# Three column groups of the input projection by seven products in a stage of their own, the second queries projected plainly, the bias table made beside x's norm

## The chip, the cores and the metric

The kernel runs on one core of one Trainium2 chip. The metric is the device time of one execution in microseconds (us), from the first to the last instruction and the little that lies around them; lower is better.

## What is computed

One transformer block on 512 tokens of width 2048, in float32. The part that matters here is the first projection and what reads it:

```python
h = rms_norm(x, norm_mix_pre)
proj = h @ w_in                       # 2048 x (q 1024, kv 6 x 256, gates 24, retention 4 x 1024)
k_cmp = compress_kv(kv6[:, :, 0], ...)   # a block MLP over 32 tokens, stride 16
v_cmp = compress_kv(kv6[:, :, 1], ...)
o_a = nsa_attention(q_a, k_cmp, v_cmp, k_slc, v_slc, k_win, v_win, gates, t5_bias)
o_r = retention(rope(q_r), rope(k_r), v_r) * silu(g_r)
mix = concat(o_a, o_r) @ w_out
x = x + rms_norm(mix); u = relu(rms_norm(x) @ w_up) ** 2; out = x + rms_norm(u @ w_down)
```

There are 8 attention heads in 2 key groups (4 heads each) and 4 retention heads. With 8 selected blocks of 64 the selected branch sees every valid key.

## The kernel before, in words

**Precision.** A float32 product is made of three fp32r matmuls: each operand is cut into a high part (a copy to fp32r on ScalarE) and a low part (source minus high part, on VectorE); `mm3` (L153 to L157) issues high x high, high x low, low x high into one PSUM bank. `split` (L141 to L144) makes the pair.

**Blocks and steps.** The projection is worked off in blocks of up to 512 output columns. A block has 8 steps (B = NSLAB = 8), one for each slab of 256 rows of the weight: a slab is fetched on the SP queue into `raw`, split into `whi`/`wlo`, and used in four pieces of six matmuls. `feat_major` (L202) keeps the weight stationary and streams 512 tokens; `tok_major` (L224) keeps the tokens stationary and streams the block's columns. Either way a block of 512 columns is 192 matmuls of 512 columns. The order of the blocks is that of `drv.steps`: the keys and values to be compressed (512 columns, `kv_done`), the selected and window keys (512, `k_done`), the first four query heads (512, `q_done(0)`), the window values (256, `v_done(1)`), then for each retention head a block of queries and keys and one of values and gates, with the last four query heads (512, `q_done(1)`) behind head 0 (L762 to L775).

**Side work.** Attention, retention and the compression are generators of small pieces, in one list (`Side`, L67; L780 to L791). Each unit has a first part (scores) and a second part (mix, outs). A call of `side.step()` makes one piece of the second part of unit b and one of the first part of a unit that may be at most one further, b + 1. The driver (L273) calls it between the pieces of a step: `two` at two of the four pieces of a step, `three` at three. A unit may wait for a block (`after(n)`: n blocks are behind). The table of L794 to L799 says up to which block the driver runs with which rate, and how many units must be through before the last step of that block: `side.drain` makes what is still missing, piece after piece, with no projection between.

```python
            if next(self.ga, "end") != "end":     # L86, first part; L97 the same for the second
                return True
    def drain(self, units=None, firsts=0):        # L106
        while self.b < (...) or self.a < firsts:
            assert self.step() or ...
```

An attention unit (`nsa_unit`, L557) takes two heads and a quarter i of the tokens (i = 0 to 3, 128 to 512 keys). Its scores are 5 pieces (6 in the last quarter): four score matmuls (L584) with scale and bias on VectorE (L585), maxima (L602 to L608), six exponentials with sums on ScalarE (L612). Its mix is i + 5 pieces: scaling of the probabilities on VectorE (L616 to L622), then for each 128 keys four transposes on TensorE (L647), their split (L648), and two pieces later the products with the values (L637). A retention unit has 10 pieces of scores and 11 of outs (L683 to L760). All engines take their instructions in the order in which they are issued.

**The rest around the change.** The stage before the blocks makes x's norm and its transposed halves `Hh`, `Hl` beside the block of selected values and gates (L400 to L435). The bias table (L453) comes as side work of the first block; `compress(0)` and `compress(1)` (L483) fetch their weights on the SP queue (L494). `load_bias` (L550) reads the table back in 8 DMAs of the POOL queue. The up and down projections already take seven products for eight (ORDER, ADD, SPLIT, `Feed`; L866 to L977): a `Feed` fetches quarters of the weight in halves of 512 KB, adds quarters on VectorE (L956) or by an accumulating DMA on POOL (L922), and splits each sum (L961 on ScalarE, L938 on VectorE); the sums of the activations are made once (`x1_sums`, L1059).

## Time and profile before

| what | value |
|---|---|
| median of 3 runs | 2201.61 us (2201.35 to 2202.2) |
| the profiled execution | 2200.95 us |
| its span, first to last instruction | 2199.0 us, 31984 instructions |
| outside the span | 1.95 us |
| mean granted TensorE clock | 0.994 |

PE is TensorE's matmuls, PEld its weight loads (they overlap matmuls), DVE VectorE, ACT ScalarE, POOL GpSimd, SP the queue that issues most DMAs. A busy PE counts every matmul from its start to its modelled end, and matmuls overlap: the pace is read from how many of them a stretch holds. L numbers are lines of the kernel before.

### The profile page before, as it was taken

The page shows a single profiled execution, that of the slowest core. Times are in us where ns is not written, and L with a number is a line of the kernel's source. Part 1 is how long each engine was busy: PE and PEld are TensorE (multiplying, and loading weights), DVE is VectorE, ACT ScalarE, POOL GpSimd, SP SyncE. Part 2 cuts the span into 40 slices and gives each one's busy share as a digit, 9 for nine tenths or more (in the row PEclk, how much of TensorE's full clock was granted, in tenths as well). Part 3 has the DMA queues.
Part 4 walks back from the last instruction along what each step waited for, and adds up shares of the span by engine and source line. Part 5 has one row for each costly group of instructions (what it writes and reads, how often), then busy time and mean ns, then how long its engine had stood idle before and what let it go on. Part 6 is the DMA issues. An engine that isn't in the chain of part 4 may idle for free.

```text
span 2199.0 us, 31984 instructions
## 1 busy us (share of the span) xinstructions
PE 2154.7 (98%) x12787; PEld 1910.5 (87%) x12787; DVE 1535.1 (70%) x1828; ACT 984.4 (45%) x1425; POOL 122.7 (6%) x139
## 2 busy tenths in 40 slices
PE   8999999999999999999999999999999999999995
PEld 7888878878788899999999999999888888888874
DVE  6213555554555533578988877777878999999996
ACT  5213343343232323485554555555664454445453
POOL 0000000000000000000000000000000000000011
PEclk9999999999999999999999999999999999999997
DMA  6543324322324334577877757676775757566684
GB/s 198 135 120 90 94 65 96 94 75 82 86 75 124 109 101 129 176 233 214 230 218 205 207 165 204 168 205 184 235 230 166 213 157 224 145 202 185 189 220 99
DMA packets 255462, 348.97 MB, mean 159 GB/s; under 512 B 16299, under 2 KB 166139, under 8 KB 254417
## 3 DMA queue, kind: packets, MB, share of 16 engines
q1 hardware_dynamic: 199472, 263.07, 38.0%
q0 software_dynamic: 29616, 42.96, 11.8%
q10 hardware_dynamic: 26226, 40.91, 5.1%
q8 instruction: 100, 1.64, 0.3%
q14 instruction: 48, 0.39, 0.1%
HBM read 305.14 MB, written 41.75 MB: 158 GB/s over the span
## 4 chain that ended last, share of the span: by engine, by line
PE 90%; DVE 5%; issue 1%; ACT 1%; DMA 1%; POOL 0%; SPq 0%; DVEq 0%; ACTq 0%; POOLq 0%
PE prod L157 17%; PE prod L155 17%; PE prod L156 17%; PE mm L155 11%; PE mm L157 11%; PE mm L156 11%; PE S L584 2%; DVE wlo L938 2%; PE PT L647 1%; PE S L707 1%; PE oT L742 1%; PE oT L502 1%; PE oT L155 1%; PE oT L156 1%; PE oT L157 1%
## 5 line engine op out<-in xcount | busy, mean ns | idle before, releaser
L961 ACT CAST whi<-Y 128x1024 fp32r<-128x1024 f32 x227 | 238.2, 1050 | 283.1 <-PE prod L157 117.6
L156 PE MATMUL prod<-wlo,Hh 128*128 128x512 f32 x896 | 349.4, 390 | 2.3 <-DVE wlo L938 2.1
L157 PE MATMUL prod<-whi,Hl 128*128 128x512 f32 x896 | 348.7, 389 | 0.0
L155 PE MATMUL prod<-whi,Hh 128*128 128x512 f32 x896 | 348.6, 389 | 0.0
L144 DVE TENSOR_TENSOR wlo<-raw,whi 128x1024 fp32r<-128x1024 f32 (+4 forms) x152 | 168.6, 1113 | 255.1 <-ACT whi L143 254.6
L961 ACT CAST whi<-low 128x1024 fp32r<-128x1024 f32 x215 | 226.4, 1054 | 265.1 <-PE prod L157 131.6
L938 DVE TENSOR_TENSOR wlo<-Y,whi 128x1024 fp32r<-128x1024 f32 x227 | 276.8, 1220 | 51.5 <-ACT whi L961 50.5
L938 DVE TENSOR_TENSOR wlo<-low,whi 128x1024 fp32r<-128x1024 f32 x215 | 262.1, 1221 | 55.9 <-ACT whi L961 55.0
L157 PE MATMUL prod<-Hh,wlo 128*128 128x256 f32 x1024 | 284.3, 278 | 5.1 <-DVE wlo L938 5.1
L155 PE MATMUL prod<-Hh,whi 128*128 128x256 f32 x1024 | 284.6, 278 | 0.3 <-ACT Hh L143 0.3
L156 PE MATMUL prod<-Hl,whi 128*128 128x256 f32 x1024 | 284.0, 277 | 0.9 <-DVE Hl L144 0.9
L143 ACT CAST whi<-raw 128x1024 fp32r<-128x1024 f32 (+4 forms) x152 | 145.6, 960 | 302.0 <-PE mm L156 147.9
L155 PE MATMUL mm<-whi,Hh 128*128 128x416 f32 (+4 forms) x704 | 262.3, 373 | 0.6 <-ACT Hh L143 0.5
L157 PE MATMUL mm<-whi,Hl 128*128 128x416 f32 (+4 forms) x704 | 248.1, 352 | 0.7 <-DVE Hl L144 0.7
L156 PE MATMUL mm<-wlo,Hh 128*128 128x416 f32 (+4 forms) x704 | 247.6, 352 | 0.0
L155 PE MATMUL mm<-Hh,whi 128*128 128x512 f32 x512 | 214.7, 419 | 0.1
L155 PE MATMUL prod<-sx,whi 128*128 128x256 f32 x768 | 212.0, 276 | 0.0
L156 PE MATMUL prod<-sx,whi 128*128 128x256 f32 x768 | 212.0, 276 | 0.0
L157 PE MATMUL prod<-sx,wlo 128*128 128x256 f32 x768 | 212.0, 276 | 0.0
L156 PEld LDWEIGHTS prod<-wlo,Hh 128*128 128x128 f32 x896 | 168.2, 188 | 40.1 <-DVE wlo L938 5.3
L157 PE MATMUL mm<-Hh,wlo 128*128 128x512 f32 x512 | 200.5, 392 | 0.0
L156 PE MATMUL mm<-Hl,whi 128*128 128x512 f32 x512 | 200.0, 391 | 0.0
(273 smaller groups left out, 3909.4 us busy)
## 6 DMA issues: line engine op xcount, KB each, us to landing
raw<-in_w_in SPq DMA_DIRECT2D x160, 256.0 KB, 3.1
low<-in_w_up SPq DMA_DIRECT2D x76, 512.0 KB, 4.3
Y<-in_w_up SPq DMA_DIRECT2D x64, 512.0 KB, 4.7
low<-in_w_down SPq DMA_DIRECT2D x64, 512.0 KB, 4.6
Y<-in_w_down SPq DMA_DIRECT2D x64, 512.0 KB, 4.6
Y<-ud SPq DMA_DIRECT2D x49, 512.0 KB, 8.0
ud<-Y ACTq DMA_DIRECT2D x77, 256.0 KB, 4.8
raw<-in_w_out SPq DMA_DIRECT2D x32, 416.0 KB, 3.5
```

The source lines that it names most:

```text
L143: nc.scalar.copy(hi, src)
L144: nc.vector.tensor_sub(lo, src, hi.bitcast(F32))
L155: nc.tensor.matmul(ps, ah, bh, start=first, stop=False, skip_group_check=more)
L156: nc.tensor.matmul(ps, ah, bl, start=False, stop=False, skip_group_check=more)
L157: nc.tensor.matmul(ps, al, bh, start=False, stop=last, skip_group_check=more)
L502: nc.tensor.matmul(hid[:65, :DK], kv[:, l:l + STRIDE * 64 + 1:STRIDE], w1s[l // 16][:, l % 16, :], start=l == 0, stop=l == CBLK - 1)
L584: nc.tensor.matmul(sps[:, :c + L], QT[g][:, h, qs], k, start=True, stop=True)
L647: nc.tensor.transpose(pt[:, e * P:(e + 1) * P], Pt[:, e, rows_of(j)], ident)
L707: nc.tensor.matmul(sps[:, :n], QK[:, 2 + d, rows_of(j)], QK[:, d, j * P:], start=d == 0, stop=d == 1)
L742: nc.tensor.matmul(o[:, :DR], AT[:, a0:a0 + P], vr[:, j, :], start=j == 0, stop=j == i)
L938: nc.vector.tensor_sub(lo, src, hi.bitcast(F32))
L961: nc.scalar.copy(hi, src)
```

## The change

The first three blocks of 512 columns (keys and values to be compressed; selected and window keys; the first four query heads) leave the list of blocks. They become a stage of their own, `groups`, between the window values and the first retention head: each group of 512 columns is two halves of 256 columns, the weight and the activations are cut in 2 x 2 quarters, and seven products of 48 matmuls of 256 columns take the place of eight. `Feed` (moved up, with parameters for its pool and offsets) feeds it. The sums of the activations are made by `in_sums`, on VectorE and ScalarE, beside the window values' block and the first products. The results go to DRAM (`pd`), and so do the values (`vd`); later they are read back on the POOL queue. The bias table is made right after the selected values. The second four query heads stay a plain block of 512, now behind retention head 1. The compression's weights go by POOL instead of SP; the list of side units and the driver's table are new. A wider tile for the split weights (`SL + 64`) and other padding go with it.

```diff
-    first = tok_outer(v0, NG * DK + 3 * HA, v_done(0))
-    kv0 = slabs_of(w_in, [(OFF_KV, 512)], pool_a)
+    first = tok_outer(v0, NG * DK + 3 * HA, v_done(0, lambda: xp.tile([P, S], F32R, name='vst')))
+    v1 = slabs_of(w_in, [(OFF_KV + 1280, 256)], pool_a)
...
     for _ in products:
         pass
+    bias_table()
     ectx.close()
+    xctx.close()
...
+    INC = [(OFF_KV, OFF_KV + 256), (OFF_KV + 512, OFF_KV + 1024), (0, 256)]
+    pd = dram.tile([len(INC), 2, P, SL], F32, name="pd")
+    iearly = [(0, 0), (1, 0), (0, 1), (1, 1), (2, 0), (0, 2), (2, 1)]
+    iphases += [(n, p, in_source(n)) for n in range(len(INC)) for p in ORDER if (n, p) not in iearly]
+    ifeed = Feed(iphases, more, 3, [], wp, in_place)
...
+        vs = [ip.tile([P, SL], F32, name="db", bufs=2)... for _ in range(2)]
+        yield from both(2, lambda c: less(vs[c], part(0, 1, c), part(1, 1, c)))
+        yield from both(4, lambda c: more_of(vs[c], sub, part(0, 0, c)))
+        yield from both(5, lambda c: more_of(vs[c], add, part(1, 0, c)))
+        yield from both(3, lambda c: less(vs[c], part(0, 0, c), part(0, 1, c)))
...
+            for s in range(2):
+                hi, lo = ifeed.slab()
+                for f in range(2):
+                    for kk in range(4):
+                        mm3(ps[:, f * 256:(f + 1) * 256], hi[:, kk, rows_of(f)], lo[:, kk, rows_of(f)],
+                            xh[:, k, :], xl[:, k, :], start, last, more)
+                    yield
...
+    drv.steps += tok_major(v1, 256, v_done(1, vst))
+    work = in_sums()
+    sums = lambda c: next(work, None) if c % 2 else None
+    drv.run(2, pump=sums)
+    drv.run(3, pump=sums)
+    ifeed.load(4)
...
+    for n, _ in enumerate(groups()):
+        if n % 2 or n % 8 == 0:
+            next(work, None)
...
-            nc.sync.dma_start(w1s[c], w1[0][c * 16 * P:(c + 1) * 16 * P, :].rearrange("(l p) n -> p l n", p=P))
+            nc.gpsimd.dma_start(w1s[c], w1[0][c * 16 * P:(c + 1) * 16 * P, :].rearrange("(l p) n -> p l n", p=P))
...
     def compress(i):
+        for _ in range(2 if i else 5):
             yield
...
         nc.scalar.copy(hs, hid[:65, :DK])
+        if not i:
+            compress_load(1)
+        else:
+            v_load()
         yield
...
+    def k_load():
+        nc.gpsimd.dma_start(kS[:, :, 32:], pd[G_K, 0].rearrange("p (g n) -> p g n", g=NG))
+        nc.gpsimd.dma_start(kW, pd[G_K, 1].rearrange("p (g n) -> p g n", g=NG))
+    def v_load():
+        for a, v in enumerate((Vh, Vl)):
+            nc.gpsimd.dma_start(v.rearrange("p t b n -> p (t b n)"), vd[a].rearrange("p t b n -> p (t b n)"))
+    def q_load():
+        QT[0] = ap.tile([P, 4, S], F32, name="qT", tag="qT")
+        for j in range(2):
+            nc.gpsimd.dma_start(QT[0][:, 2 * j:2 * j + 2, :].rearrange("p f n -> p (f n)"), pd[G_Q0, j])
...
-    drv.steps += feat_major(kv0, 4, kv_done)
-    proj([(OFF_KV + 512, 256), (OFF_KV + 1024, 256)], k_done)
-    proj([(0, 512)], q_done(0))
-    proj([(OFF_KV + 1280, 256)], v_done(1), tok=True)
     for h in range(HR):
         proj([(OFF_QR + h * DR, DR), (OFF_KR + h * DR, DR)], qk_done(h))
         proj([(OFF_VR + h * DR, DR), (OFF_GR + h * DR, DR)], vg_done(h), tok=True)
-        if h == 0:
-            proj([(512, 512)], q_done(1))
+        if h == 1:
+            proj([(512, 512)], q_done)
     B = NSLAB
     two = lambda c: side.step() if c % 2 else None
     three = lambda c: side.step() if c else None
+    every = lambda c: side.step()
     after = lambda n: (lambda: drv.at > n * B)
-    side.add(bias_table, nothing)
-    side.add(lambda: compress(0), nothing, after(1))
-    side.add(lambda: compress(1), nothing, after(1))
+    def loads():
+        k_load()
+        load_bias(0)
+        q_load()
+        for _ in range(6):
+            yield
+    side.add(lambda: compress(0), nothing)
+    side.add(lambda: compress(1), nothing)
+    side.add(loads, nothing)
     for u in range(8):
-        side.add(*nsa_unit(0, u // 2, u % 2), after(3), after(4))
-    side.add(*ret_unit(0), after(6))
+        if u == 4:
+            side.add(*ret_unit(0), after(2), after(3))
+        side.add(*nsa_unit(0, u // 2, u % 2))
+    side.add(*ret_unit(1), after(4), after(5))
     for u in range(8):
-        side.add(*nsa_unit(1, u // 2, u % 2), after(7))
-        if u == 5:
-            side.add(*ret_unit(1), after(9))
-    side.add(*ret_unit(2), after(10), after(11))
-    side.add(*ret_unit(3), after(12))
-    for blocks, units, firsts, pump in ((3, 3, 0, two), (4, 0, 0, two), (7, 10, 11, three), (8, 11, 12, three),
-                                        (9, 12, 12, three), (10, 12, 19, two), (11, 19, 19, two),
-                                        (12, 22, 22, three)):
+        if u == 4:
+            side.add(*ret_unit(2), after(7), after(8))
+        side.add(*nsa_unit(1, u // 2, u % 2), after(6))
+    side.add(*ret_unit(3), after(9))
+    kv_load()
+    compress_load(0)
+    for blocks, units, firsts, pump in ((2, 0, 0, every), (3, 0, 0, three), (4, 7, 8, three), (5, 8, 0, three),
+                                        (6, 11, 12, three), (7, 12, 13, three), (8, 13, 0, three), (9, 22, 22, three)):
         drv.run(blocks * B - 1, pump=pump)
         side.drain(units, firsts)
```

In the changed list the window values are block 0; the retention heads' and the second queries' blocks are 1 to 9 (queries and keys of head 0, its values and gates, the same of head 1, the second queries as block 5, then heads 2 and 3), and the output projection starts with block 10.

## Rows read from the trace of the kernel before

**Rows 1.** The page's first part (busy time, share of the span and number of instructions of each engine) and a group of weight loads from its fifth (count, then busy us, mean ns of one | idle before).
```profile
PE 2154.7 (98%) x12787; PEld 1910.5 (87%) x12787; DVE 1535.1 (70%) x1828; ACT 984.4 (45%) x1425; POOL 122.7 (6%) x139
...
L156 PEld LDWEIGHTS prod<-wlo,Hh 128*128 128x128 f32 x896 | 168.2, 188 | 40.1 <-DVE wlo L938 5.3
```
**Rows 2.** Busy time by stage (stretches): x's norm; the three blocks and the compression; the window values; the nine blocks with the side work; the output projection; up; down. Columns: stretch, its length, then busy us and (instructions) of each engine, granted clock, DMA share, GB/s.
```profile
0.00:48.80 48.80, 39.68 (x261) 35.23 (x262) 33.72 (x64) 28.61 (x66) 4.82 (x12) 1.00 0.63 202
48.80:198.60 149.80, 149.80 (x722) 123.53 (x721) 35.08 (x51) 31.96 (x44) 5.28 (x10) 1.00 0.44 118
198.60:222.70 24.10, 24.08 (x209) 23.88 (x207) 10.94 (x28) 11.62 (x36) 0.00 (x0) 1.00 0.43 121
222.70:749.90 527.20, 526.47 (x2485) 423.59 (x2486) 294.20 (x551) 182.97 (x393) 12.91 (x24) 1.00 0.32 90
749.90:936.70 186.80, 185.74 (x1021) 184.19 (x1020) 86.39 (x128) 67.97 (x126) 7.69 (x14) 1.00 0.42 129
936.70:1560.10 623.40, 617.38 (x5409) 616.44 (x5410) 504.66 (x504) 348.70 (x433) 42.80 (x36) 1.00 0.72 203
1560.10:2174.00 613.90, 611.55 (x2690) 503.66 (x2688) 560.59 (x487) 306.91 (x320) 42.22 (x36) 1.00 0.64 189
```
**Rows 3.** What the matmuls of the whole span waited for: us in total, times, longest.
```profile
PE prod L157 <- DVE wlo L938: 5.1, 3, 3.8
PE mm L331 <- DMA g<-in_norm_mix_pre: 3.9, 1, 3.9
PE PT L339 <- DVE h L355: 3.9, 3, 2.1
PE prod L156 <- DVE wlo L938: 2.1, 4, 1.2
PE oT L742 <- DVE rn L748: 0.7, 1, 0.7
```
**Rows 4.** Two stretches of 100 us with one shape of matmul each: 256 columns (up) and 512 columns (down); columns as in rows 2.
```profile
1200.00:1300.00 100.00, 100.00 (x883) 100.00 (x882) 80.35 (x82) 54.46 (x65) 7.63 (x6) 1.00 0.72 199
1700.00:1800.00 100.00, 100.00 (x443) 82.81 (x442) 94.57 (x83) 48.51 (x49) 7.09 (x6) 1.00 0.68 202
```
**Rows 5.** VectorE's groups of instructions in the up stage (936 to 1560 us), by shape: busy us, mean ns of one | idle before.
```profile
L938 DVE TENSOR_TENSOR wlo<-Y,whi 128x1024 fp32r<-128x1024 f32 x112 | 136.6, 1222 | 38.5 <-ACT whi L961 37.6
L956 DVE TENSOR_TENSOR Y<-Y,low 128x1024 f32<-128x1024 f32 x35 | 42.7, 1219 | 0.2
L1074 DVE TENSOR_TENSOR Y<-Y 128x1024 f32<-128x1024 f32 x8 | 9.7, 1218 | 0.0
```
**Rows 6.** VectorE's group of the window values' slabs (48.8 to 222.7 us), by shape.
```profile
L144 DVE TENSOR_TENSOR wlo<-raw,whi 128x512 fp32r<-128x512 f32 x8 | 5.5, 690 | 15.5 <-ACT whi L143 15.5
```
**Rows 7.** DMA issues of the whole program: queue, count, KB each, median us from issue to landing.
```profile
low<-in_w_up POOLq DMA_DIRECT2D x21, 512.0 KB, 7.6
BT<-rd POOLq DMA_DIRECT2D x16, 128.0 KB, 6.9
w1s<-in_cmp_w_k SPq DMA_DIRECT2D x2, 0.5 KB, 7.8
```
**Rows 8.** Two stretches by what the DMA engines did: the compression's second weights, and the bias read back beside a block's slabs; columns as in rows 2.
```profile
135.00:145.00 10.00, 10.00 (x50) 8.16 (x49) 1.23 (x1) 1.13 (x2) 0.00 (x0) 1.00 0.99 300
160.00:171.00 11.00, 11.00 (x52) 8.78 (x50) 3.19 (x9) 1.20 (x2) 3.98 (x8) 1.00 0.89 159
```
**Rows 9.** The POOL engine's groups of issues, of the whole span: busy us, mean ns of one | idle before.
```profile
L922 POOL DMA_DIRECT2D low<-in_w_up x21 | 26.7, 1272 | 319.6 <-ACT whi L961 132.1 <-DVE Y L956 82.4 <-DVE low L956 59.2
L553 POOL DMA_DIRECT2D BT<-rd x16 | 8.1, 515 | 280.0 <-DVE Pt L585 177.2 <-PE oT L502 102.8
L442 POOL DMA_DIRECT2D hot<-in_c_hot x1 | 0.6, 632 | 0.3 <-issue 0.3
```
**Rows 10.** One mix of the last quarter in order of time (start us, us, engine line operation), beside the scores of the next unit; the block's matmuls between them are left out.
```profile
608.00 0.18 DVE L616 RECIPROCAL nst<-nst 128x6 f32<-128x6 f32 x1
608.22 0.17 DVE L618 TENSOR_TENSOR nst<-nst,gat 128x6 f32<-128x6 f32 x1
608.42 1.68 DVE L622 TENSOR_SCALAR Pt<-Pt,nst 128x512 f32<-128x512 f32 x4
...
614.68 0.60 PE L647 MATMUL PT<-misc,Pt 128*128 128x128 f32 x4
615.12 1.02 PE L584 MATMUL S<-kT,qT 128*128 128x512 f32 x2
615.32 0.59 ACT L143 CAST ph<-PT 128x512 fp32r<-128x512 f32 x1 [2.50 <-PE PT L647]
615.93 0.69 DVE L144 TENSOR_TENSOR pl<-PT,ph 128x512 fp32r<-128x512 f32 x1 [1.61 <-ACT ph L143]
```
**Rows 11.** ScalarE's exponentials of the last quarter and the reads of their sums (400 to 749.9 us), by shape.
```profile
L612 ACT ACTIVATION_READ_ACCUMULATOR Pt<-Pt,nst 128x1 f32 x32 | 6.0, 186 | 0.0
L612 ACT ACTIVATE Pt<-Pt,nst 128x512 f32<-128x512 f32 x8 | 5.7, 710 | 0.0
L612 ACT ACTIVATE Pc<-Pc,nst 128x31 f32<-128x31 f32 x4 | 1.2, 311 | 0.0
```
**Rows 12.** VectorE's maxima of the last quarter and TensorE's side matmuls (500 to 749 us and 222.7 to 749.9 us), by shape.
```profile
L608 DVE TENSOR_REDUCE nst<-Pt 128x2 f32<-128x1024 f32 x2 | 2.4, 1220 | 0.1
L155 PE MATMUL oT<-ph,Vh 128*128 128x256 f32 x80 | 22.5, 281 | 0.0
```
**Rows 13.** A long wait of TensorE at the start of the up stage, and the stretch behind it; columns as in rows 2.
```profile
990.00:994.30 4.30, 0.48 (x5) 0.28 (x3) 4.30 (x5) 2.25 (x3) 0.71 (x1) 1.00 1.01 326
994.30:998.70 4.40, 4.40 (x25) 4.40 (x26) 4.38 (x4) 2.50 (x4) 1.92 (x2) 0.61 0.83 203
```

More of the change, by code (lines that the diff above doesn't have):

```diff
@@ L265, in block_kernel, with __init__, add, step @@
+    class Later:
+        def __init__(self):
+            self.at, self.todo = 0, []
+        def add(self, slabs, work):
+            self.todo.append((self.at + slabs, work))
+        def step(self):
+            self.at += 1
+            due = [w for n, w in self.todo if n <= self.at]
+            self.todo = [(n, w) for n, w in self.todo if n > self.at]
+            for w in due:
+                w()
     side = Side()
@@ L315, in block_kernel @@
     xts, hx, sx = {}, {}, {}
-    ones = ap.tile([1, P], F32, name="ones")
+    ones = xp.tile([1, P], F32, name="ones")
     nc.vector.memset(ones, 1.0)
@@ new lines, in groups @@
+    def groups():
+        sets = []
+        for i, (g, p, _) in enumerate(iphases):
+            n = g if isinstance(g, int) else g[0]
+            more = p in (1, 6)
+            if more:
+                ps = held_in.pop((n, p))
+            else:
+                ps = mm.tile([P, S], F32, name="mm")
+                if p in (0, 3):
+                    held_in[n, {0: 1, 3: 6}[p]] = ps
+            for s in range(2):
+                hi, lo = ifeed.slab()
+                if s == 0 and sets:
+                    in_done(*sets.pop())
+                ilater.step()
+                hi, lo = (v.rearrange("p (k n) -> p k n", k=4) for v in (hi, lo))
+                xh, xl = IA[p]
+                for f in range(2):
+                    for kk in range(4):
+                        k = 4 * s + kk
+                        o = ps[:, f * 256:(f + 1) * 256]
+                        start, last = k == 0 and not f and not more, k == 7 and f == 1
+                        mm3(o, hi[:, kk, rows_of(f)], lo[:, kk, rows_of(f)], xh[:, k, :], xl[:, k, :], start, last,
+                            more)
+                    yield
+            sets.append((n, p, ps))
+        yield
+        in_done(*sets.pop())
+        for _ in range(3):
+            ilater.step()
@@ new lines, in block_kernel, with vst @@
+    vsts = []
+    def vst():
+        if not vsts:
+            v = ip.tile([P, SL], F32R, name="vst", tag="da", bufs=3)
+            vsts.extend((v[:, :S], v[:, S:]))
+        return vsts.pop(0)
+    drv.steps += tok_major(v1, 256, v_done(1, vst))
[4 more added lines that the diff above has]
+    ifeed.load(4)
+    drv.run(len(drv.steps) - 2, pump=sums)
+    raws = [wr.tile([P, KC, S], F32, name="raw").rearrange("p k n -> p (k n)") for _ in range(3)]
@@ new lines, in block_kernel @@
+    ifeed.free += raws
+    for _ in range(3):
+        ifeed.advance()
+    drv.run(len(drv.steps) - 1, pump=sums)
+    drv.run()
+    next_up = slabs_of(w_in, [(OFF_QR, DR), (OFF_KR, DR)], pool_a)
+    for n, _ in enumerate(groups()):
+        if n % 2 or n % 8 == 0:
+            next(work, None)
+        if raws and not ifeed.loads and all(any(r is f for f in ifeed.free) for r in raws):
+            for i in range(3):
+                next_up[i].fetch()
+            raws = []
+        if ifeed.at == 2 * len(iphases) and not hasattr(next_up[0], "hi"):
+            next_up[0].load()
@@ L833, in block_kernel @@
     for s in range(NSLAB):
-        drv.run(12 * B + s + 1, pump=lambda c: side.first() if c % 2 else None)
+        drv.run(9 * B + s + 1, pump=lambda c: side.first() if c % 2 else None)
         if s:
@@ L839, in block_kernel @@
     mx.close()
-    drv.run(14 * B - 1, pump=lambda c: side.second() if c % 2 else None)
+    drv.run(11 * B - 1, pump=lambda c: side.second() if c % 2 else None)
     side.drain()
-    drv.run(16 * B)
+    drv.run(13 * B)
     rctx.close()
@@ L1128, in block_kernel @@
     phases += [(("down", c, nb), p, dn_source(c, nb)) for c in range(NCH) for nb in range(2) for p in ORDER]
-    feed = Feed(phases, [low0, low1], 3, [("down", NCH - 1, nb) for nb in range(2)])
+    feed = Feed(phases, halved(low0) + halved(low1), 3, [("down", NCH - 1, nb) for nb in range(2)], hp,
+                lambda g, p, s: 40 if isinstance(g, int) and p == 6 and s else 0)
     tmp = Ring(*xt, *(xh[:, c:c + 512] for c in range(0, 2048, 512)))
```

398 lines of the change are left out of this document (234 added, 164 removed).

## The prediction

> **What bounds the kernel now.** I read the page's first part, then the stages, then what TensorE waited for. Matmuls fill 98% of the span [rows 1], and between 48.8 and 2174 us no stage leaves TensorE idle by more than a per cent [rows 2]. In the nine blocks with the side work the only wait of a matmul that shows is 0.7 us, of a retention product; the longest of all lie at the starts of the norm and of the up stage [rows 3]. So attention's long chains cost TensorE's own time and nothing more: a piece always has a block's matmuls around it. The time therefore falls by what TensorE is spared, and rises by every place where it has to wait.
>
> **What the seven products save.** Three blocks are 3 x 192 = 576 matmuls of 512 columns; the new stage has 3 x 7 x 48 = 1008 of 256. Where one shape runs alone, 100 us hold 443 wide matmuls, 225.7 ns each, or 883 narrow ones, 113.3 ns each [rows 4]. 576 x 0.2257 = 130.0 us against 1008 x 0.1133 = 114.2 us: **15.8 us saved**. The old stage of 149.8 us [rows 2] is this 130.0 and the compression and table, which stay.
>
> The Trainium skill (TensorE: Matmul & The Clock Gate, section Back-to-back issue gap) speaks against this: it gives sustained spacings of 81 ns at 128 columns and 131 ns at 512. An estimate on a straight line between them is 98 ns at 256, so 98 us for the new stage against 75 for the old, a loss of 23 us, and a sum of 2257. The trace disagrees with that page: its narrow matmul costs half a wide one.
>
> **The sums of the activations.** `in_sums` is 28 VectorE pieces on 1024 elements, 1.22 us each as such pieces of the up stage [rows 5]. 16 lie beside the window values' block, whose 192 narrow matmuls last 21.7 us. VectorE owes in that time 16 x 1.22 = 19.5, six low parts of slabs at 0.69 = 4.1 [rows 6], two first low parts of the new stage, 2.4, and four low parts of values, about 1.7: 27.7 us. The third slab's low part ends at 28.9 and is wanted at 21.7 + 2 x 2.7 = 27.1, 1.8 us late. For the next five products a slab (24 matmuls, 2.7 us) carries one low part and 1.25 pieces, 2.75 us, so the delay neither grows nor shrinks much. The nearest row for such a start is that of the up stage, whose products waited 5.1 + 2.1 us for low parts [rows 3]. Bounds 0 and 7; I take **+4**, between the hand count and that row.
>
> **The read back.** Keys, queries and values were copied from PSUM into place; now they come from DRAM through POOL's queue, in issue order. `v_load` goes out with call 20 of the side work (13 pieces of `compress(0)`, 7 of `compress(1)`), `k_load`, the bias and `q_load` with call 24, and the first score matmul with call 30. One call per six matmuls: the cover is 10 x 6 x 0.2257 = 13.5 us. Ahead of the first queries lie 2.1 MB of values, 1.05 of keys, 1.05 of bias and 0.52 of queries. DMA engines that are full moved 300 GB/s; the bias took 11 us beside a block's slabs at 159 GB/s in all [rows 8], its issues 0.5 us each [rows 9], 6.9 us to landing [rows 7]. A block's slabs are 4.2 MB in 43 us, 97 GB/s, which leaves some 200. Upper end: 3.67 / 0.2 = 18.4, and 11 for the bias, less 13.5: 16. Lower end: all 4.7 MB at 300 GB/s, 15.7 less 13.5: 2. TensorE takes instructions in order, so this wait holds up the block behind it too. I take **+10**: the bias's slow pace is measured on this very transfer, while the slabs are fetched up to three ahead and can give way. The first compression's weights (1.05 MB each, 7.8 us to landing [rows 7]) have six to eight calls, 8 to 11 us, of cover; bounds 0 and 4, taken as 0.
>
> **The drain.** This is what decides. I walked the driver's loop call by call. In the old table every unit due at a `drain` is through: no piece is ever left over. In the new one nine blocks instead of twelve carry the side work, and two of them carry less than they could: in block 5 11 of 24 calls find nothing (the second queries are not there yet), in block 7 9 (head 2's outs wait for block 8). At block 8 the line is head 2's outs, 11 pieces; unit 14's mix, 7; unit 15's mix. 21 calls come before the drain, and 11 + 7 + 3 = 21. Left are 4 pieces of unit 15's mix, then 8 of unit 16's, one call for unit 16's change to unit 17, and 8 of unit 17's, with the scores of 16 and 17 beside them: **21 steps with no block's matmul between**, on the widest units there are.
>
> What TensorE waits for in them: from a unit's last score to its first transposition there are one maximum, 1.22 us [rows 12], six exponentials with the reads of their sums, 4 x (0.710 + 0.186) + 2 x (0.311 + 0.186) = 4.6 us [rows 11], and the scaling, 2.1 us [rows 10]: 7.9 us, with some 3 us of the other unit's pieces beside it. Twice, about 10 us. In the other pieces transpositions, high part and low part take 1.94 us (614.68 to 616.62) [rows 10], then six products of about 0.118 us (pace of the narrow matmul; 281 ns each if alone [rows 12]): 2.6 us for the two pieces that may be in flight, 1.3 each, against about 1.0 of TensorE's own. 0.3 x 20 = 6. Together **+16**. Lower end 8, when only one of the long waits shows; upper end 28, when no two pieces are in flight (14 x 1.3 = 18, and 10).
>
> **The clock.** A wait of 3.8 us in the up stage was followed by 4.4 us with a granted clock of 0.61, most of it at the lower of the two levels (1.2 of 2.4 GHz), holding 25 matmuls where the pace of rows 4 gives 39: 1.6 us lost [rows 13]. Three waits here are as long or longer. 3 x 1.6 = 4.8, but in the drain TensorE is not the bound: **+3**, bounds 0 and 5.
>
> **At nothing.** The bias table keeps its three products; its issues on POOL (0.6 us each [rows 9]) stand in front of the last root of x's norm there, under the selected values' products, 1.7 us if that cover is gone. The late sums are issues of 1.27 us on POOL [rows 9], 7.6 us to landing [rows 7], with three products, 16 us, ahead of their use. 36 halves of 0.52 MB, 3.1 MB of accumulation and 3.1 of stores in about 118 us are 213 GB/s, beside 203 at a DMA share of 0.72 in the up stage [rows 2]. SP, relieved of the compression's weights, had made nothing wait.
>
> **Sum.** Against the profiled execution's 2200.95 us (span 2199.0 and 1.95 around it; the median, 2201.61, is 0.7 higher): 2200.95 - 15.8 + 4 + 10 + 16 + 3 = **2218 us**.
>
> **Rivals.**
> 1. *The loads are hidden, the drain is not.* The number of empty calls of `compress` and `loads` speaks for it, the bias's 11 us against. Without the 10 and one clock drop: 2207. Chance 0.20.
> 2. *Faster: the leftover pieces run at TensorE's pace.* The place is the end of block 8. Unit 15's remainder and unit 16's pieces would have to cover unit 17's exponentials, and the loads to land in time; the price is then 2200.95 - 15.8 + 4 + 1 = 2190. It decides when the idle time of the drain and of the first score together stays under 10 us. For it: VectorE is busy for 56% of these blocks and ScalarE for 35% [rows 2]. Against: the chain is one of latencies, and needs 7.9 us whatever else is idle. Chance 0.11.
> 3. *The new stage starves.* Each group wants four halves at its second product, from eight buffers; in the up stage's start the long wait came with the DMA engines full, 326 GB/s [rows 13]. Three times 3.8 + 1.6 in place of 4: 2218 + 12 = 2230. Chance 0.08.
> 4. *The weight load paces the narrow matmul.* It is busy 100% of the narrow stretch, 83% of the wide [rows 4], and takes 188 ns [rows 1]. If two could not overlap: 1008 x 0.188 = 190 us, 2218 + 75 = 2293. 883 in 100 us exclude it where it was measured: 0.01. The spacings of the Trainium skill's page named above would be a milder form of it.
>
> **How the numbers follow.** The forecast has 0.59. The range, 2200 to 2238, reaches down over the first rival and the low ends and up over the third; below it lies most of the second, above it the sum of the upper ends (2241) and the fourth. A measurement of this kernel can tell some 0.2%, 4.4 us, from no change. Faster by more: rival 2, 0.12 with a remainder. Within: the lower half of rival 1, 0.10. Slower: the forecast, the upper half of rival 1, rivals 3 and 4, 0.78.
>
> **What would show it.** Right: the stage of the 1008 products lasts 114 to 122 us; a wait of TensorE of 5 to 15 us before the first L584-like score, released by a DMA; two waits of 4 to 6 us ahead of transpositions at the end of block 8, released by VectorE, and in that stretch a busy share near 0.6 and a dip of the granted clock. Wrong: a first score that waits under 2 us (rival 1); no stretch without block matmuls, or one under 25 us (rival 2); more than 10 us of waits for low parts in the new stage (rival 3).

## The result: slower by 1.1%

| | before | after |
|---|---|---|
| median of the compared runs | 2201.9 us (2201.35 to 2202.65, 4 runs) | 2226.72 us (2222.95 to 2228.86, 4 runs) |
| profiled execution, its span | 2200.95, 2199.0 us | 2225.34, 2222.9 us |

The ratio of the two versions' times is 1.0111, 95% interval [1.0093, 1.0128]. The profiled execution is 24.4 us longer than before; the forecast was 17 us. The saving came as predicted, the costs were larger and lay in part in other places.

The page's first part after, to be held against [rows 1]: TensorE has 432 instructions more, VectorE 82 us more to do, and the span grew.

```profile
PE 2156.9 (97%) x13219; PEld 1929.1 (87%) x13219; DVE 1617.3 (73%) x1907; ACT 1009.4 (45%) x1448; POOL 149.1 (7%) x171
```

The stages after, against [rows 2]: the norm, the window values, a short stretch at the new stage's start, the three groups, the nine blocks (the compression now in them), up, down; the output projection, left out, is as long as before. Columns as there: stretch, length, busy us and (instructions) of PE, PEld, DVE, ACT, POOL, granted clock, DMA share, GB/s.

```profile
0.00:49.50 49.50, 41.44 (x261) 37.12 (x262) 33.03 (x65) 27.88 (x66) 7.05 (x15) 1.00 0.63 188
49.50:72.90 23.40, 23.40 (x198) 22.29 (x197) 19.42 (x25) 7.88 (x12) 1.40 (x2) 1.00 0.81 233
72.90:78.00 5.10, 0.29 (x4) 0.09 (x2) 4.65 (x6) 4.03 (x7) 0.00 (x0) 0.79 0.68 209
78.00:196.90 118.90, 117.44 (x1009) 117.05 (x1010) 94.47 (x90) 49.72 (x53) 15.51 (x18) 0.98 0.73 191
196.90:770.90 574.00, 557.95 (x2640) 447.05 (x2640) 304.36 (x588) 190.40 (x424) 25.09 (x44) 0.98 0.36 104
...
957.70:1582.80 625.10, 618.83 (x5409) 617.89 (x5410) 504.94 (x504) 349.01 (x434) 42.98 (x36) 0.99 0.72 203
1582.80:2197.40 614.60, 611.78 (x2688) 503.43 (x2687) 560.50 (x487) 306.86 (x320) 42.45 (x36) 1.00 0.65 188
```

How the spans' 23.9 us come out of these stages. Before, everything from the norm's end to the output projection took 749.9 - 48.8 = 701.1 us; after, 770.9 - 49.5 = 721.4, so 20.3 more. The saving of 15.8 is in it, so 36.1 us were added. Values and groups should have taken 24.1 + 114.2 = 138.3 and took 147.4: **9.1**. Compression, table and nine blocks took 149.8 - 130.0 + 527.2 = 547.0 before, the last two of them 574.0 after: **27.0**. The other 3.6 us are 0.7 in the norm, 1.7 in up, 0.7 in down and 0.5 behind the last stage.

What the matmuls waited for, over the whole span, the longest groups (total, times, longest), against [rows 3]:

```profile
PE PT L973 <- DVE Pt L948: 5.5, 2, 3.1
PE prod L157 <- DVE wlo L339: 5.4, 3, 3.8
PE mm L155 <- DVE vst L144: 4.8, 1, 4.8
PE oT L813 <- ACT KV L809: 4.2, 1, 4.2
...
PE oT L1068 <- DVE rn L1074: 3.1, 4, 1.5
```

The `prod` waits are the up stage's, as before. Three others are new and long: 4.8 us for the values' split `vst`, 4.2 us for a copy into `KV`, and 5.5 us in two for the scaled probabilities `Pt` (L948 is L622 of the kernel before). No score (L910) waits long, neither for a DMA nor at its first place.

**The saving.** In the middle of the groups, one shape of matmul with its sums beside it:

```profile
115.00:175.00 60.00, 60.00 (x531) 60.00 (x530) 49.05 (x47) 24.50 (x25) 5.05 (x4) 1.00 0.79 212
```

531 in 60 us is 113.0 ns each, the up stage's pace of [rows 4]. The stage's 118.9 us are the 114.2 of the forecast, 1.5 of waits for low parts, 2.4 lost at its start, where 4.7 us of work ran at half the clock, and 0.8 that I cannot place.

**The start of the groups.** Around the 4.8 us wait, in order of time (start us, us, engine line operation, tiles, shape, count, [idle before <- releaser]); the value block's last matmul starts at 72.90:

```profile
72.43 2.35 DVE L339 TENSOR_TENSOR wlo<-half,whi 128x1024 fp32r<-128x1024 f32 x2
...
73.21 1.04 ACT L362 CAST whi<-half 128x1024 fp32r<-128x1024 f32 x1 [1.81 <-PE mm L157]
...
74.16 1.99 ACT L656 CAST sv<-db 128x1024 fp32r<-128x1024 f32 x2
75.23 2.36 DVE L658 TENSOR_TENSOR sv<-db,sv 128x1024 fp32r<-128x1024 f32 x2 [0.45 <-ACT sv L656]
76.06 1.19 ACT L143 CAST vst<-mm 128x256 fp32r<-128x256 f32 x4
77.51 1.41 DVE L144 TENSOR_TENSOR vst<-mm,vst 128x256 fp32r<-128x256 f32 x4
```

The first product of the groups needs a PSUM bank that still holds values. They were finished at 73 us, but ScalarE first made a slab half's high part and those of two sums (L656), VectorE the low parts of two halves and of the sums (L658), and only then came the values' own pair at 76.06 and 77.51; TensorE goes on at 77.98. The clock fell while it stood:

```profile
72.90:75.90 3.00, 0.28 (x3) 0.08 (x1) 2.55 (x3) 2.69 (x3) 0.00 (x0) 1.00 0.45 113
75.90:82.70 6.80, 4.71 (x22) 4.72 (x23) 6.80 (x10) 1.34 (x5) 2.84 (x4) 0.50 0.95 269
```

**The first compression.** ScalarE at 210 us, its next two instructions after one that ended at 200.3; L143 makes the high parts of the blocks' slabs, L809 copies the positions beside the keys, and TensorE's product L813 reads them:

```profile
209.99 1.04 ACT L143 CAST whi<-raw 128x1024 fp32r<-128x1024 f32 x1 [9.73 <-DMA raw<-in_w_in]
210.94 0.18 ACT L809 COPY KV<-PT 128x32 f32<-128x32 f32 x1
```

The first row is the point. ScalarE takes instructions in order; the cast stands for 9.7 us because its slab has not landed, and the copy behind it, whose input was there at 205.3, waits too. What the DMA engines did meanwhile, from the DMA view of 194 to 212 us (a queue with packets, MB and share of the engines' time; issues with KB each and median us to landing):

```profile
q0 software_dynamic: 1145, 3.79, 63.3%
...
w1s<-in_cmp_w_k POOLq DMA_DIRECT2D x2, 1024.0 KB, 15.5
raw<-in_w_in SPq DMA_DIRECT2D x6, 256.0 KB, 13.2
```

The queue fed by POOL takes 63% of the engines' time. The weights need 15.5 us, where [rows 7] had 7.8; a slab of 256 KB needs 13.2, where the whole program's median is 3.1. That POOL's transfers are what makes the slab late is the nearest reading and is not shown (experiments 7 and 10). The clock again, in the last part of the wait and behind it (columns as in the stages):

```profile
209.00:211.20 2.20, 0.03 (x1) 0.03 (x1) 0.13 (x1) 1.13 (x2) 0.00 (x0) 0.50 1.05 297
211.20:215.80 4.60, 4.60 (x19) 4.41 (x20) 1.09 (x1) 0.00 (x0) 0.00 (x0) 0.50 0.85 259
```

**The read back.** POOL's issues of bias and queries, in order of time:

```profile
247.52 4.25 POOL L879 DMA_DIRECT2D BT<-rd  x8 [18.41 <-PE oT L813]
251.77 1.11 POOL L867 DMA_DIRECT2D qT<-pd  x2
```

The bias stands for a tile that the second compression's products (L813) still read; keys and values had gone out at 226.8 to 229. The half of the queries that the first score reads lands 9.8 us after its issue, at 261.6, and that score starts at 262.5.

**The drain.** The end of block 8 in five stretches, cut where the clock changes: up to the end of the first wait, what follows it, up to the end of the second, what follows that, and the rest. Columns as above:

```profile
683.90:690.30 6.40, 3.32 (x20) 2.25 (x18) 4.71 (x10) 4.27 (x14) 0.00 (x0) 1.00 0.01 3
690.30:697.10 6.80, 6.77 (x15) 3.39 (x16) 3.85 (x11) 1.17 (x2) 0.00 (x0) 0.50 0.06 19
697.10:707.10 10.00, 6.60 (x40) 4.88 (x40) 6.69 (x13) 5.23 (x16) 0.00 (x0) 1.00 0.00 0
707.10:713.90 6.80, 6.63 (x27) 5.52 (x28) 3.43 (x8) 1.76 (x3) 0.00 (x0) 0.52 0.06 19
713.90:719.60 5.70, 5.36 (x31) 4.45 (x30) 1.56 (x3) 2.85 (x5) 0.00 (x0) 0.98 0.09 25
```

For 35.7 us no block matmul runs (DMA share near 0: no slab is fetched). TensorE is idle for 7.0 of them, and twice 6.8 us pass at half the clock, with 13.4 us busy; at the upper level, I estimate, that work would have taken 6.7. In the second row it is busy 6.77 us with 15 matmuls: a full busy column beside a granted clock of 0.50 is work at half speed, no gain. A score behind the first wait takes 2.08 us for two matmuls where [rows 10] shows 1.02:

```profile
691.88 2.08 PE L910 MATMUL S<-kT,qT 128*128 128x512 f32 x2
```

### The profile page after: what moved, and what is told of

Read it like the earlier page. It is cut to its first block, busy times and chain, and to the rows that moved or that the text cites. A ratio compares the mean times of both kernels' runs of the same rounds, so it can differ in the third digit from the quotient of the medians.

```text
span 2222.9 us, 33079 instructions
## 1 busy us (share of the span) xinstructions
PE 2156.9 (97%) x13219; PEld 1929.1 (87%) x13219; DVE 1617.3 (73%) x1907; ACT 1009.4 (45%) x1448; POOL 149.1 (7%) x171
## 4 chain that ended last, share of the span: by engine, by line
PE 83%; DVE 8%; DMA 4%; issue 2%; ACT 2%; POOL 0%; SPq 0%; ACTq 0%; DVEq 0%; POOLq 0%
PE prod L157 16%; PE prod L156 16%; PE prod L155 16%; PE mm L155 9%; PE mm L157 9%; PE mm L156 9%; DMA raw<-in_w_in 2%; DVE wlo L339 2%; PE S L910 2%; PE PT L973 1%; PE S L1033 1%; PE oT L813 1%; PE oT L1068 1%; DMA half<-in_w_in 1%; PE oT L155 1%
## 5 line engine op out<-in xcount | busy, mean ns | idle before, releaser
L144 DVE TENSOR_TENSOR wlo<-raw,whi 128x1024 fp32r<-128x1024 f32 (+4 forms) x128 | 139.1, 1092 | 188.7 <-ACT whi L143 188.2
L143 ACT CAST whi<-raw 128x1024 fp32r<-128x1024 f32 (+4 forms) x128 | 120.2, 943 | 224.3 <-PE mm L157 100.1
L157 PEld LDWEIGHTS prod<-Hh,wlo 128*128 128x128 f32 x1024 | 193.6, 189 | 6.1 <-DVE wlo L339 6.0
L155 PEld LDWEIGHTS prod<-whi,Hh 128*128 128x128 f32 x896 | 168.2, 188 | 35.0
L157 PEld LDWEIGHTS prod<-whi,Hl 128*128 128x128 f32 x896 | 168.2, 188 | 34.5
```

The lines of the kernel that those rows point to most:

```text
L143: nc.scalar.copy(hi, src)
L144: nc.vector.tensor_sub(lo, src, hi.bitcast(F32))
L155: nc.tensor.matmul(ps, ah, bh, start=first, stop=False, skip_group_check=more)
L157: nc.tensor.matmul(ps, al, bh, start=False, stop=last, skip_group_check=more)
```

## The experiments

All are made from the kernel after, and ratios are to the kernel before, measured beside each. The names in brackets are those by which the expectations call them. The executions of one version lie 2 to 7 us apart, so the difference of two versions' medians is known to some 3 us; smaller ones are read from the traces, each of a single execution. Experiments 8 and 9 leave the positions out of the first compression, so that the part of their copy in the wait can be seen.

**1 (e1). Fewer pieces left for the drain.** Retention head 2's unit goes two places later in the side list, which fills calls of blocks 7 and 8 that found nothing.

```diff
-        if u == 4:
+        if u == 6:
             side.add(*ret_unit(2), after(7), after(8))
```

> Head 2's unit of retention moves behind two more attention units, so that 7 steps instead of 21 are left for the drain before the last step of block 8 (unit 17's scores end and its mix). Theory 1 (a leftover piece costs TensorE's waiting, not its own work): one of the two long waits and the shorter waits of 14 pieces go, 8 to 12 us of some 17, so 2215 to 2219 us, ratio to the kernel before about 1.007. Rival (the pieces cost TensorE the same wherever they stand): 2224 to 2229, ratio 1.011 as the changed kernel.

Measured: 2211.91 us (2211.23 to 2213.54), ratio 1.0046 [1.0029, 1.0062]: 14.8 us under the kernel after, more than expected. The nine blocks, whole, and the place where the first wait was:

```profile
195.90:755.90 560.00, 550.13 (x2641) 441.78 (x2640) 304.03 (x588) 189.92 (x424) 25.07 (x44) 1.00 0.37 107
684.00:700.00 16.00, 15.28 (x86) 12.42 (x85) 8.36 (x16) 7.57 (x20) 0.00 (x0) 1.00 0.25 74
```

574.0 became 560.0, so the gain is all in this stage; both long waits and both stretches at half clock are gone. The drain's idle time of 7.0 and the 6.7 lost to its clock make 13.7. The match with 14.0 is not quite so close: some 1.4 of the 14.0 lie at the first compression, which this edit leaves alone (a wait of 3.4 us here for 4.2, and 3.4 us at the lower clock for 6.8), and against it stands a new wait of 1.0 us before a score. The drain's cost is shown, by an edit that changes no arithmetic.

**2 (e2). No piece left.** As 1, and block 9's pump given all calls in the place where `three` skipped one in four.

```diff
-        ..., (8, 13, 0, three), (9, 22, 22, three)):
+        ..., (8, 13, 0, three), (9, 22, 22, every)):
```

> As the run with 7 steps left, and in block 8 a piece at each of the four parts of a step: nothing is left at the drain. Theory 1: the whole cost of the drain goes, 16 us as predicted and 1 to 3 of the lower clock, so 2207 to 2211 us, ratio 1.003, and no stretch without a block's matmuls; the same pieces are hidden elsewhere. Rival: no more than 3 us less than the changed kernel, ratio 1.010, because VectorE and ScalarE then delay the block's own slabs.

Measured: 2215.82 us (2212.12 to 2217.24), 1.0059 [1.0044, 1.0074]. Not the further gain expected: 3.9 over experiment 1, about as much as can be told. TensorE's waits of the last blocks (600 to 765 us) fit that; in experiment 1 these two lines have 1.0 us each there. That a piece at every call asks for a chain's next link too soon is my reading of them.

```profile
PE oT L1068 <- DVE rn L1074: 3.8, 2, 2.6
PE S L910 <- DVE Pt L911: 1.7, 2, 1.1
```

**3 (e7). No piece left, the room taken elsewhere.** Retention head 2 at `u == 7`, and `(7, 12, 13, three)` made `every`; block 9 stays as it was.

> Head 2's unit stands behind three more attention units and block 6, whose units are the narrowest, takes a piece at each of the four parts of a step; block 8 keeps three. Nothing is left at the drain. Theory 1 (a leftover piece costs about 1 us, and the run with none left lost part of it again to a fuller block 8, where retention's and attention's chains waited): 2205 to 2211 us, ratio 1.002 to 1.004, below the run with 7 left; waits in blocks 7 and 8 under 4 us together. Rival (7 leftover pieces cost nothing more once the widest unit's exponentials are covered): 2211 to 2214, as the run with 7 left.

Measured: 2212.63 us (2208.72 to 2214.99), 1.0041 [1.0027, 1.0055], as experiment 1 within the spread. So seven leftover pieces cost nothing that can be measured beside none, as the rival had it; it was the two long waits and the clock behind them that cost. Its nine blocks:

```profile
196.70:757.30 560.60, 550.59 (x2640) 442.49 (x2639) 303.99 (x588) 190.14 (x424) 25.09 (x44) 0.99 0.36 106
```

This kernel is the base of experiments 6 to 11.

**4 (e3). The sums laid out otherwise.** 10 of the 28 pieces beside the values in place of 14, none in that block's last steps, and the rest in three of four products of the groups.

```diff
-    drv.run(len(drv.steps) - 2, pump=sums)
+    drv.run(5, pump=sums)
+    drv.run(len(drv.steps) - 2)
...
-    drv.run(len(drv.steps) - 1, pump=sums)
...
-        if n % 2 or n % 8 == 0:
+        if n % 4 != 3:
```

> Only the sums of the activations are spread: 10 instead of 14 pieces beside the window values' block, and three pieces in four parts instead of five in eight beside the first five products. Everything else as in the changed kernel. Theory 2 (the first product waits 4.8 us for a PSUM bank whose values VectorE splits too late, behind its backlog of sums, and the lower clock for 6.8 us behind it takes 2 to 3 more): 2218 to 2222 us, ratio 1.008, the wait of 5.1 us under 1. Rival (what is late are the halves of the weight, the wait moves to the low parts of the first slabs): 2225 to 2229, ratio 1.011.

Measured: 2220.68 us (2219.19 to 2221.64), 1.0083 [1.0068, 1.0098]: 6.0 under the kernel after. The wait for the values' split shrank, though not to under 1 us, and the clock stayed up behind it:

```profile
PE mm L155 <- DVE vst L144: 1.9, 1, 1.9
```
```profile
75.00:82.00 7.00, 7.00 (x62) 7.00 (x63) 6.39 (x8) 4.39 (x6) 2.83 (x4) 1.00 1.07 292
```

62 matmuls in 7 us is the full pace, where the kernel after had 22 in 6.8. Values and groups take 142.5 us in this trace, where they took 147.4: some 5 of the 9.1 us hung on how the sums stand in the queues of two engines, and 4.2 stayed.

**5 (e6). The first score earlier.** Is the read back of keys, bias and queries hidden by luck? Experiment 2 with one empty call behind the loads in place of six.

```diff
         q_load()
-        for _ in range(6):
+        for _ in range(1):
             yield
```

> As the run with nothing left, but the empty calls between the issue of the queries' read and the first score go from 6 to 1: 5 x 1.36 = 6.8 us less cover. Theory 3 (the queries land when the POOL queue has issued the bias behind the second compression's last matmul, some 14 us later, and the first score sits just at that time): TensorE waits 6 to 8 us before the first score and loses 2 to 3 at the lower clock, so 7 to 11 us more than the run with nothing left. Rival (they land earlier, the cover was not used): within 1 us of it.

Measured: 2219.84 us (2219.31 to 2225.83), 1.0086 [1.0071, 1.0101], 4.0 over experiment 2, where 7 to 11 were expected.

```profile
PE S L910 <- DMA qT<-pd: 4.8, 1, 4.8
```

The wait that I had forecast appears, by a DMA and at the first score, when five calls of cover are taken away. 6.8 us of cover less and 4.8 of wait leave 2 us to spare in experiment 2; in the kernel after it was 0.9 (261.6 against 262.5). The read back is hidden, but narrowly.

**6 (e8). More cover for the first compression.** Experiment 3 with nine empty calls ahead of it in place of five.

```diff
-        for _ in range(2 if i else 5):
+        for _ in range(2 if i else 9):
```

> The run before this one, and nine instead of five empty calls ahead of the first compression. Theory 4 (its first product waits 4 us because ScalarE, in order, sits at the cast of a slab that lands 14 us after its issue, and the copy of the position code stands behind that cast): four calls, 5.4 us, cover it; the wait and the 3.4 to 6.8 us of lower clock behind it go, 5 to 7 us less than the run before this one. Rival (the slab itself is late for its own step, so TensorE waits there): within 1.5 us of it.

Measured: 2208.72 us (2205.19 to 2212.07), 1.0026 [1.0015, 1.0036]: 3.9 less than experiment 3, where 5 to 7 were expected, and a wait of 2.7 us for the same copy was left. By then ScalarE stood at the next late slab:

```profile
213.44 1.04 ACT L143 CAST whi<-raw 128x1024 fp32r<-128x1024 f32 x1 [3.77 <-DMA raw<-in_w_in]
214.39 0.18 ACT L809 COPY KV<-PT 128x32 f32<-128x32 f32 x1
```

**7 (e9). Less ahead of it.** Experiment 3 with two transfers, some 1 MB, moved in the program behind the compression: the rotation table and the second half of the read back of `KV`.

```diff
-    nc.gpsimd.dma_start(rot, c_rot)
...
+            kv_load(1)
             compress_load(1)
```

> The run with nothing left and block 6 fuller, with five empty calls, but the rotation table and the values to be compressed (0.5 MB each) are read later on the POOL queue. Theory 4 (the slab is late because the POOL queue's 3.6 MB go ahead of it in full DMA engines): 1 MB less at 300 GB/s brings the slab 3 us earlier, the wait of 4 us shrinks to 0 to 1.5, and 3 to 6 us are saved. Rival (the slab waits for its buffer, or for SP, not for bandwidth): no change.

Measured: 2211.74 us (2210.14 to 2213.81), 1.0039 [1.0024, 1.0054]: no gain, and the wait (4.6 us) is no shorter. But the edit did half of what it was meant to. POOL's issues of the two:

```profile
195.77 0.57 POOL L783 DMA_DIRECT2D KV<-pd  x1
230.65 0.54 POOL L1105 DMA_DIRECT2D rot<-in_c_rot  x1
```

The second half of `KV` still left 17 us ahead of the compression's first product, right behind the weights: POOL issues when what an issue waits for is free, whatever the call. So half a megabyte less, and another half behind the weights, did not bring the slab sooner (ScalarE stood 10.1 us for it, 9.3 in experiment 3), while the weights landed in 12.1 us, not 15.2. A megabyte less was not tried.

**8 (e11). Without the copy.** Is it ScalarE's order, or are the weights as late?

```diff
-        pt = bank("PT", 2)
-        nc.tensor.transpose(pt[:, :CBLK], pes, ident[:CBLK, :CBLK])
-        nc.scalar.copy(kv[:, NG * S:], pt[:, :CBLK])
+        if i:
+            ...
```

> The kernel of e7 without the transposition and ScalarE copy of the positions in the first compression (its position column is zero; nothing else is left out). In e7 the first compression product waited 3.8 us for that copy, which stood on ScalarE behind the cast of a slab that landed at 209.3 us; but the first half of the compression's weights, too, landed only at about 208.5 us (issued 195.0, 13.5 us to landing), two microseconds after it was wanted. Theory (ScalarE's order is the wait, the weights are right behind it): the wait no longer ends at ScalarE, a wait of 1.5 to 2.5 us for the weights' DMA takes its place, and the time is 1.5 to 3 us below e7's 2212.6: 2210. Rival (the weights and not the copy set it, the copy only came last by a hair): a wait of 3.5 to 4.5 us stays, now ended by a DMA, and the time stays at 2212 to 2213.

Measured: 2207.58 us (2205.56 to 2212.26), 1.0028 [1.0018, 1.0037], 5.0 under experiment 3; the intervals of the two ratios overlap.

```profile
PE oT L816 <- DMA w1s<-in_cmp_w_k: 1.6, 1, 1.6
```
```profile
207.80:212.00 4.20, 4.20 (x31) 3.94 (x32) 1.23 (x1) 1.05 (x1) 0.00 (x0) 1.00 1.07 306
```

Both were late, the copy by more. Without it the weights end the wait, 2.2 us sooner, as expected; and the clock stays at its upper level behind this shorter wait, where experiment 3 has 3.4 us at the lower one, 1.7 lost. By the traces that is 3.9; the rest of the 5.0 can't be told from noise.

**9 (e13). Without the copy, nine calls.**

> The same with nine empty calls ahead of the first compression in place of five (the kernel of e8 without the position copy). The weights then have until about 212 us. Theory: in e8 the 2.7 us left were again the copy behind a late slab's cast (213.4 us), so here the first compression product waits for nothing (under 0.5 us), and the time is 2.5 to 4.5 us below e8's 2208.7: 2205. Rival (the DMA engines are full and whatever is wanted first is late): a block's own matmul or the weights wait 2 to 3 us in its place, 2208 to 2209.

Measured: 2206.37 us (2204.37 to 2207.81), 1.0015 [1.0007, 1.0024]: 6.3 under experiment 3. No wait of the first compression product is left. Against experiment 6 it is 2.4 less, about the 2.7 us of that one's wait, though that difference alone is no more than the noise. That this place costs some 6 us, and that it is the copy behind the cast and then the weights that TensorE stands for, is shown; why slab and weights land late is not.

**10 (e12). The weights on SP's queue again.** One part of the change undone, on experiment 3.

```diff
-            nc.gpsimd.dma_start(w1s[c], w1[0]...)
+            nc.sync.dma_start(w1s[c], w1[0]...)
```

> The kernel of e7 with one part of the change undone: the compression's weights on SP's queue again, as before, in place of POOL's. Their issues then stand behind six slabs on SP, which wait for free buffers. Theory (DMA engines that are full for 20 us, whichever queue carries what): the slabs ahead land sooner (under 10 us), the weights later than 209 us, and the first compression product waits 3 to 7 us, now for the weights' DMA; 2212 to 2217. Rival (a bulk transfer in POOL's queue is what slows the slabs and itself; on SP these weights took 7.8 us in the kernel before): weights and slabs land in under 9 us, no wait over 1 us at the compression, 2206 to 2208.

Measured: 2216.29 us (2212.79 to 2218.25), 1.0060 [1.0046, 1.0074]. The time came as my theory had it, by another way. SP's issues (start, us in which the group was issued) and ScalarE's next two:

```profile
191.08 2.01 SPq L176 DMA_DIRECT2D raw<-in_w_in  x4
193.55 6.79 SPq L799 DMA_DIRECT2D w1s<-in_cmp_w_k  x2
200.44 9.71 SPq L176 DMA_DIRECT2D raw<-in_w_in  x4
```
```profile
213.86 1.04 ACT L143 CAST whi<-raw 128x1024 fp32r<-128x1024 f32 x1 [11.63 <-DMA raw<-in_w_in]
214.81 0.18 ACT L809 COPY KV<-PT 128x32 f32<-128x32 f32 x1
```

The weights go out behind four slabs, not six, and the slab that ScalarE wants is now behind the weights: ScalarE stands 11.6 us for it, 9.3 in experiment 3, and the wait for the copy is 5.5 us, 3.8 there. I had the weights' DMA ending it. The rival, that POOL's queue as such is slow, falls: on SP these weights took 17.4 us.

**11 (e10). All three costs together.** Experiment 3, the sums of 4, the transfers as in 7 and seven empty calls.

> All together: nothing left and block 6 fuller, the later reads, seven empty calls, and the sums spread (10 pieces beside the window values, three in four parts behind). If the three costs add: the changed kernel's 2226 less about 17 (drain), 6 (sums) and 6 (compression): 2195 to 2201 us, ratio 0.997 to 1.000, that is some 5 us of the 15.8 saved stay. If they share their cost (the lower clock counted twice): 2201 to 2206.

Measured: 2200.53 us (2197.77 to 2203.13, 10 runs) against 2202.76 (2201.18 to 2207.33, 18 runs), ratio 0.9988 [0.9978, 0.9997]: the one version under the kernel before, by 0.1%, which is at the edge of what can be told. Values, groups, nine blocks:

```profile
50.70:75.00 24.30, 22.43 (x194) 22.10 (x194) 18.98 (x24) 8.86 (x14) 1.34 (x2) 1.00 0.84 247
75.00:193.20 118.20, 115.95 (x1009) 115.14 (x1010) 98.79 (x94) 51.84 (x56) 15.59 (x17) 1.00 0.76 201
193.20:745.50 552.30, 546.68 (x2640) 440.13 (x2639) 303.60 (x588) 189.78 (x424) 24.93 (x44) 1.00 0.36 107
```

The clock is at its upper level in all three. Of the added 36.1 us, 9.5 are left here: 0.2 with the values, 4.0 in the groups, where products wait 2.2 us for low parts, and 5.3 in the nine blocks. The norm is 1.9 longer than before. So 11.4 of the 15.8 still go there. At the compression 0.6 us of wait is left, with seven calls, where experiment 6 had 2.7 with nine; which of the other edits does that was not tried.

## Why the prediction was right or wrong

**The saving: right.** 113.0 ns for a matmul of 256 columns, forecast 113.3. The milder form of rival 4, the spacings of the Trainium skill (TensorE: Matmul & The Clock Gate, section Back-to-back issue gap), gave 98 ns as an estimate for that width and more for this stage than for the old one; the run disagrees, as the rows of before did.

**The sums of the activations: too small, 4 for 6.7, and 2.4 of clock behind.** The step priced VectorE's backlog as waits for low parts of slabs, and those were 1.5 us. It left out whose turn it is at the hand-over: the values' own pair, which frees the bank, stands behind two sums on ScalarE and on VectorE. It also counted 16 pieces beside that block, where the driver's last step has no pump and 14 run. Rival 3, a starving stage, did not happen: no DMA wait shows in the groups.

**The read back: the wrong place, 10 for none at the first score; 4.2 came at the compression, with 2.3 of clock behind.** The step let `loads` be issued by its call number and took the calls as cover. On POOL an issue goes when what it waits for is free: keys and values left long before, and of what followed the bias only the queries had to land before 262.5. In that rival 1 was right, by the prediction's own sign of a first score that waits under 2 us. The full DMA engines that it feared were there, 50 us earlier, where the first compression's weights and the read back of `KV` meet the first slabs. That place I had "at nothing", with bounds 0 and 4, and asked only whether the weights land. What landed late was also a slab, and TensorE met it through a copy queued behind that slab's cast on ScalarE. Here the step failed: a shared engine's order carried a delay from one transfer to a reader of another.

**The drain: right in place, and in size by luck.** 16 forecast for 21 leftover steps; 14 of them taken away gave 14.8. But the 16 were waits of TensorE alone, two of about 5 us and 6 us of small ones, and the waits were 7.0 us in all, the two long ones 3.1 and 2.5; TensorE was busy for 28.7 of the 35.7 us, 0.80 and not near 0.6. Another 6.7 us went to the clock, which I had reckoned nearly free there because "TensorE is not the bound". At half clock it was: the second row of the drain has it busy 6.77 of 6.80 us.

**The clock: mis-sized, 3 for some 13.** [rows 13] had 4.4 us at a mean of 0.61 and a loss of 1.6 us. After, four new stretches at 0.50 to 0.52 lie behind waits, of 6.8 us each: 2.4 us lost at the groups' start, some 2.3 at the compression (19 matmuls in the 4.6 us behind the wait), 6.7 in the drain. The up stage's own stretch was longer as well, with the same waits ahead of it, and that is enough for the 1.7 us by which the stage grew:

```profile
1014.50:1021.30 6.80, 5.49 (x25) 5.49 (x26) 5.89 (x6) 3.83 (x5) 2.64 (x2) 0.50 0.92 218
```

It is 6.8 us at half clock where [rows 13] has 4.4 at 0.61, 3.4 of them at the lower level. Ten of the eleven experiments have 3.4 here again, so this 1.7 belongs to the execution and not to the change. One row was no measure of such a stretch.

**What I had not seen.** The outs of retention wait 3.1 us in all for VectorE (L1068), 0.7 before. Experiments 2, 3 and 11 move these 3 us about and don't remove them. The 27.0 us of the nine blocks are 15.3 of more idle time (574.0 less 557.95 busy, less the 0.7 of before), 9.0 lost to the clock and 2.7 besides. The idle time is 4.2 at the compression, 7.0 in the drain, 2.4 of these outs, and 1.7 in smaller waits of the compression's second layer and of a score. In experiment 3, where no piece is left for the drain, the same count (10.0 idle and two stretches of 3.4 us at half the clock in 560.6) leaves 0.9 besides. So some 2 us of the drain are neither idle time nor clock, and that part stays open.

So 17 us were forecast and 24.4 came: costs of 33 forecast, and 39.7 in the spans. In the prediction's terms the saving was as forecast; the sums cost 6.7 for 4, the read back 4.2 in another place for 10, the drain's waits 7.0 for 16, the clock 13 for 3; nearly 9 us more had no term. That the sum came near owes something to luck: what was too high in the read back and the drain made up for most of what was missing in the clock and elsewhere.

## What to carry to other kernels

Before merging or dropping blocks that carry side work, count the pieces and the calls: what is left over runs without cover, and moving one unit two places was worth 14.8 us. For every transfer put beside others, ask not only when its reader needs it but what its neighbour's lateness blocks: an engine that waits in order for one slab holds up every small copy queued behind. Price a new wait of some microseconds between busy matmul stretches at half as much again or more, since the clock may fall behind it: 4.8 cost 2.4 beside it, 4.2 cost 2.3, and the drain's 7.0 of idle time 6.7. It is a price with a spread: behind the same 4.8 us experiments 1 and 6 have 3.4 us at the lower level, and lose 1.6.

## What the runs showed that I had not expected

- Behind the compression's wait of 4.2 us the clock was at its lower level, behind one of 1.6 us at the same place (experiment 8) it stayed at the upper; the same at the groups' start with 4.8 and 1.9 us (experiment 4). In the drain it fell with a wait of 2.45 us that had other short gaps ahead of it. And one wait of 2.2 us for retention's outs, at the same place in experiments 3 and 6 to 11, was followed by 3.4 us at the lower level in four of these seven traces and by none in three.
- The same wait at the same place in the up stage was followed by 4.4 us at 0.61 in one kernel and 6.8 us at 0.50 in another, with 25 matmuls in either.
- With POOL's queue moving 3.8 MB in 18 us, slabs on SP's queue took 13.2 us to land and not 3.1, and taking half a megabyte of it away (experiment 7) did not bring the awaited slab sooner; putting the weights on SP made them 17.4 us and that slab later.
- POOL's issues left long ahead of the place that the program gives them: in experiment 7 the second half of `KV`, written behind the first compression, went out 17 us ahead of that compression's first product.
